# Two-pass scores on the full array, values of a token tile in one row, compression in one row with its weights in the stream's buffers

## The chip, the cores and the metric

One core of a Trainium2 chip runs the whole kernel in one launch. The metric is the device time in microseconds (us): the median of several executions, smaller is better. The engines named here are TensorE (PE, with its weight loads as PEld), VectorE (DVE), ScalarE (ACT) and SyncE (SP), which issues the DMAs of the weights.

## What is computed

Two layers of a decoder trunk on 256 tokens of width 1024, in float32. Each layer projects the normalized tokens with one wide matrix `w_in`, lets two attention mixers (NSA and DSA) work on the result, adds their output to the residual, and ends with a SwiGLU block. Cut to what the change touches:

```python
def layer(x):                                   # SEQ 256, D 1024, twice
    proj = rmsnorm(x) @ w_in                    # nsa_q, k/v for cmp/slc/win, dsa q/k/v, index q/k, gates
    # NSA: 8 heads of 64 in 2 groups; rope on q and keys
    kc = gelu(blocks(k_cmp) @ cmpk_w1 + b1) @ cmpk_w2 + b2   # 15 blocks of 32 tokens, w1: 2048 x 128
    vc = gelu(blocks(v_cmp) @ cmpv_w1 + b1) @ cmpv_w2 + b2
    o_c, o_s, o_w = softmax(q @ kc.T) @ vc, softmax(q @ k_slc.T) @ v_slc, softmax(q @ k_win.T) @ v_win
    # DSA: index scores pick 64 keys for each token, then 8 heads of 64
    sel = topk(sum(relu(iq @ ik.T) * iw), 64)
    o_d = softmax(dsa_q @ dsa_k[sel].T) @ dsa_v[sel]
    x = x + (gate_n * (o_nsa @ w_branch_nsa) + gate_d * (o_d @ w_branch_dsa)) @ w_out
    h = rmsnorm(x)
    return x + (silu(h @ w_ffn_gate) * (h @ w_ffn_up)) @ w_ffn_down
```

## The kernel before

**Weight stream.** All large matrices pass through `weights()` (L158 to L168). SP loads a piece of 128x1024 floats (512 KB) into `raw`, a pool of five buffers; ACT rounds it into `hi` (L164), DVE subtracts it from the piece into `lo` (L165), both in pools of four. `mul3` (L173 to L175) then multiplies each half of the split weights in three passes (hi by hi, hi by lo, lo by hi): twelve matmuls of 512 columns for a piece, L173, L174 and L175 in turn. A `raw` buffer comes free when its `lo` has been made. SP issues in one queue, in the order of the program, so an issue that waits holds back all behind it.

**Order.** A scheduler lays the matmuls of the attention between those of the stream. In each layer the order of the stream around the change is: index queries and keys, keys and values of NSA, queries of NSA (`nq`, column 0 of `w_in`), then the DSA queries (dq, four pieces of `w_in`), the DSA keys (dk, four), the DSA values (dv, four), then the gates.

**Scores.** `split` writes the hi part of queries and keys into plane 0 and the lo part into plane 1 of `qs` and `ks` (L315 to L318). `pair` (L320 to L325) computes two heads at a time, one on rows 0 to 63 of the array and one on rows 64 to 127: three passes each, so six matmuls that contract over 64 rows, of 256 columns (index scores, DSA, the first token tile of NSA) or 512 (second tile of NSA).

**Values.** `values` in `nsa` (L595) and in `dsa` (L636) multiplies the transposed weights `pt` with the values, 64 columns of the array for each of two heads. With `LAG = 1` the values of one group of heads are issued after the softmax of the next one.

**Compression.** The hidden layer of both compressions (L505) goes through four strips of 32 columns of the array (keys and values, first and second half of the contraction). Eight loads of 256 KB `w1` (L503) have a pool of their own of three buffers; after each come four matmuls on one strip. `blk`, the gathered blocks, comes from the NSA projections.

Of the kernel before, what the change touches and what calls it, by code (L numbers as in the profile page):

```python
# [9 lines left out]
F32 = mybir.dt.float32  # L10
# [19 lines left out]
WARM = 11  # L30
LAG = 1
HALF = (slice(0, 64), slice(64, 128))
PTB = 5

# [45 lines left out]
def hybrid_trunk(ctx: ExitStack, tc: tile.TileContext, a: dict, out: bass.AP):  # L80
# [233 lines left out]

    def split(dst, src):  # L315

        nc.scalar.activation(dst[0], src, AF.Copy)
        nc.vector.tensor_sub(dst[1], src, dst[0].bitcast(F32))  # L318

    def pair(outs, q, k):  # L320


        for n, (a, b) in enumerate(((0, 0), (0, 1), (1, 0))):
            for e in range(2):
                nc.tensor.matmul(outs[e], q[a][HALF[e]], k[b][HALF[e]], start=n == 0, stop=n == 2)  # L325

# [16 lines left out]
    for l in range(DEPTH):  # L343
# [16 lines left out]

        ks = one.tile([P, 2, NT, 2 * P], F32R, tag="ks", name="ks")
        qs = one.tile([P, 2, 4, SEQ], F32R, tag="qs", name="qs")
# [26 lines left out]
        iqs = one.tile([P, 2, 4, SEQ], F32R, tag="qs", name="iqs")[:, :, :, 0:P]  # L389
        iks = one.tile([P, 2, NT, 2 * P], F32R, tag="ks", name="iks").rearrange("p a b t -> p a (b t)")[:, :, 0:SEQ]  # L390
        for i in range(NT):
            nc.vector.tensor_scalar_mul(iw[:, i], pji[:, i, 576:584], 512 ** -0.5)
            rope(pji[:, i, 0:576].rearrange("p (h d) -> p h d", d=64), i, (9,))
            nc.vector.tensor_copy(pji[:, i, 576:640], pji[:, i, 512:576])
            tok = slice(i * P, (i + 1) * P)
            qp = tr_bank()
            for k in range(4):
                nc.tensor.transpose(qp[:, k * P:(k + 1) * P], pji[:, i, k * P:(k + 1) * P], ident)
            q3 = qp.rearrange("p (k t) -> p k t", t=P)
            if i == 0:  # L400
                iqT = work.tile([P, 4, P], F32, tag="pr", name="iqT", bufs=8)
                nc.scalar.activation(iqT, q3, AF.Copy)
            else:
                split([iqs[:, a] for a in range(2)], q3)
            kp = tr_bank()[:, 0:P]
            nc.tensor.transpose(kp, pji[:, i, 512:640], ident)
            nc.scalar.activation(iks[:, 0, tok], kp, AF.Copy)
            if i == 0:
                nc.scalar.activation(ikT, kp, AF.Copy)
            nc.vector.tensor_sub(iks[:, 1, tok], kp, iks[:, 0, tok].bitcast(F32))  # L410
        for i in range(NT):
# [4 lines left out]
            for p0 in range(0, 4, per):  # L416
                sbs = [sc_bank() for _ in range(2)]
                for p in range(p0, p0 + per):
                    outs = [sb[:, (p - p0) * nk:(p - p0 + 1) * nk] for sb in sbs]
                    if i == 0:  # L420
                        for e in range(2):
                            nc.tensor.matmul(outs[e], iqT[HALF[e], p], ikT[HALF[e]], start=True, stop=True)
                    else:
                        pair(outs, [iqs[:, z, p] for z in range(2)], [iks[:, z] for z in range(2)])
                for e in range(2):
                    rl = work.tile([P, 512], F32, tag="k2", name="rl", bufs=3)
                    nc.scalar.activation(rl, sbs[e], AF.Relu)
                    for p in range(p0, p0 + per):
                        h = 2 * p + e
                        nc.vector.scalar_tensor_tensor(acc, rl[:, (p - p0) * nk:(p - p0 + 1) * nk],  # L430
                                                       iw[:, i, h:h + 1], prev, ALU.mult, ALU.add)
                        prev = acc
# [13 lines left out]
        for c0, n in ((512, 512), (1024, 280), (0, 512)):  # L446
            d = project(act, w_in, c0, n)
            for i in range(NT):
                if c0 == 0:
                    nq[i] = work.tile([P, 512], F32, tag="q2", name="nq", bufs=4)  # L450
                    evac(nq[i].rearrange("p (r g d) -> p r g d", r=4, g=2),
# [5 lines left out]
        for i in range(NT):  # L457
# [13 lines left out]
            for k, c in enumerate((C_KSLC, C_KWIN)):  # L471
                nc.tensor.transpose(kp[:, k * P:(k + 1) * P], pj[:, i, c - C0:c - C0 + P], ident)
            split([ks[:, z, i] for z in range(2)], kp[:, 0:2 * P])
            tok = slice(i * P, (i + 1) * P)
# [4 lines left out]
            nc.scalar.activation(qT[:, :, tok], q3, AF.Copy)  # L479
            split([qs[:, z, :, tok] for z in range(2)], q3)  # L480
            nc.scalar.activation(eg[:, i], pj[:, i, C_NG - C0:C_NG - C0 + 24], AF.Exp, scale=-1.0)
            nc.vector.tensor_scalar(eg[:, i], eg[:, i], 1.0, None, ALU.add)


        hp = sc_bank()
        for kind, nm in ((0, "cmpk"), (1, "cmpv")):
            blk = work.tile([P, 16, 32], F32, tag="pr", name="blk", bufs=8)
# [3 lines left out]
            for half in range(2):  # L491
                src = kvP[:, kind].rearrange("p g (c m) -> p m g c", m=8)[:, :, :, half:half + 15]
                po = cols[:, pos + half * 8:pos + half * 8 + 8].unsqueeze(2).broadcast_to((P, 8, 15))
                for g in range(2):
                    nc.vector.tensor_add(blk4[:, half * 8:(half + 1) * 8, g, 0:15], src[:, :, g], po)
            for half in range(2):
                q = 32 * (2 * half + kind)
                for mq in range(2):
                    r0 = half * 1024 + mq * 512
                    w1 = work.tile([P, 4, P], F32, tag="w1", name="w1", bufs=3)  # L500
                    if l == 0 and kind == 0 and half + mq < 2:
                        after(w1[:, 0, 0:1], pji[:, 0, 0:1])
                    nc.sync.dma_start(w1, a[nm + "_w1"][l, r0:r0 + 512].rearrange("(m p) h -> p m h", p=P))  # L503
                    for m in range(4):
                        nc.tensor.matmul(hp[q:q + 32, 0:P], blk[:, half * 8 + mq * 4 + m], w1[:, m],  # L505
                                         start=mq == 0 and m == 0, stop=mq == 1 and m == 3, tile_position=(0, q))
        hs = work.tile([P, P], F32, tag="hs", name="hs", bufs=1)
# [31 lines left out]
        for c0, dst in ((C_DQ, dqT), (C_DK, dkT), (C_DV, None)):  # L539
            d = project(act, w_in, c0, 512)  # L540
            for i in range(NT):
                if dst is None:
                    evac(dv[:, i], d[i], rstd[i])
                    continue
                q = work.tile([P, 512], F32, tag="q2", name="dq", bufs=4)
                evac(q, d[i], rstd[i])
# [11 lines left out]
        def nsa(i):  # L558
# [30 lines left out]

            def values(r0, pts):  # L590
                for r in range(r0, r0 + per):
                    for kind, vcol in ((0, C_VSLC - C0), (1, C_VWIN - C0)):
                        for b in range(i + 1):
                            for g in range(2):
                                nc.tensor.matmul(yn[g * 64:(g + 1) * 64, r * P:(r + 1) * P],  # L595
                                                 pj[:, b, vcol + g * 64:vcol + g * 64 + 64],
                                                 pts[g][:, ((r - r0) * 2 + kind) * (i + 1) + b],
                                                 start=r == 0 and kind == 0 and b == 0, stop=False)

            done = []  # L600
            for r0 in range(0, 4, per):
# [3 lines left out]
                for r in range(r0, r0 + per):  # L605
                    pair([o[r - r0] for o in outs], [qs[:, z, r, tok] for z in range(2)],
                         [ks[:, z, 0:i + 1].rearrange("p b t -> p (b t)") for z in range(2)])
                for g in range(2):
# [6 lines left out]
                done.append((r0, pts))  # L615
                if len(done) > LAG:
                    values(*done.pop(0))
            for d in done:
                values(*d)
            for r in range(4):  # L620
# [4 lines left out]
        def dsa(i):  # L625
# [4 lines left out]

            def values(p0, pts):
                for p in range(p0, p0 + per):
                    for b in range(i + 1):
                        for e in range(2):
                            v0 = (2 * p + e) * 64
                            nc.tensor.matmul(yd[e * 64:(e + 1) * 64, p * P:(p + 1) * P], dv[:, b, v0:v0 + 64],  # L636
                                             pts[e][:, (p - p0) * (i + 1) + b], start=p == 0 and b == 0,
                                             stop=p == 3 and b == i)

            done = []  # L640
            for p0 in range(0, 4, per):
                pts = []
                sbs = [sc_bank() for _ in range(2)]
                for p in range(p0, p0 + per):
# [4 lines left out]
                    else:  # L649
                        pair(outs, [dqs[:, z, p] for z in range(2)], [dks[:, z, p] for z in range(2)])  # L650
                for sb in sbs:
                    segs = sb.rearrange("p (h b t) -> p h b t", h=per, t=P)
                    pts.append(softmax([segs[:, h] for h in range(per)], dbias[i], None))
                done.append((p0, pts))
                if len(done) > LAG:
                    values(*done.pop(0))
            for d in done:
                values(*d)
            y_out(yd, 4, tok)
# [4 lines left out]
        dks = one.tile([P, 2, 4, SEQ], F32R, tag="qs", name="dks")  # L664
        dqs = one.tile([P, 2, NT, 2 * P], F32R, tag="ks", name="dqs").rearrange("p z b (c t) -> p z (b c) t", t=P)
        split([dks[:, z] for z in range(2)], dkT)
        split([dqs[:, z] for z in range(2)], dqT[:, :, P:])
        dsa(0)
# [190 lines left out]
```

## Time and profile before

| | |
|---|---|
| median of 3 runs | 834.9 us (834.82 to 835.3) |
| profiled execution | 835.01 us, span of its trace 833.0 us |
| mean granted TensorE clock | 0.999 |
| PE busy | 824.6 us, 99% of the span |
| DVE busy | 534.0 us, 64% |
| ACT busy | 452.4 us, 54% |
| PE's share of the chain that ended last | 98% |

The span is what the trace covers; 2.0 us of the profiled execution lie outside it. Busy shares are averages over the span; a row of the timeline is one instruction, or several alike in a row, with its start and its length. Ends of matmuls are modelled, so lengths of neighbours overlap, and what an instruction costs PE is read from start to start.

### The profile page before, as it was taken

Reading aid. Unit: us, or ns where it says so; the run is one execution under the profiler, and the core shown is the slowest. Engines: PE = TensorE matmul, PEld = TensorE weight load, DVE = VectorE, ACT = ScalarE, POOL = GpSimd, SP = SyncE. Lnnn points to the kernel's source line nnn. Section 1 sums busy time; section 2 is a strip of 40 time slices with the busy share of each in tenths; the row PEclk is TensorE's granted clock in tenths of the full one; section 3 lists DMA queues with packets and bytes.
Section 4 is the critical chain, followed back from the end, with each engine's and each line's share of the span. In section 5 each row is a group of like instructions: output and inputs, shape, how many; then the busy total and the mean of one; then the engine's idle time right before and its main releaser. Section 6 shows DMA issues by size and latency. Waiting matters only on the chain.

```text
span 833.0 us, 12280 instructions
## 1 busy us (share of the span) xinstructions
PE 824.6 (99%) x4501; PEld 680.1 (82%) x4501; DVE 534.0 (64%) x1163; ACT 452.4 (54%) x777; POOL 8.4 (1%) x18
## 2 busy tenths in 40 slices
PE   8999999999999999999999999999999999999997
PEld 7878887778888888988898888777788888889886
DVE  6699478868665556554668956767577555556445
ACT  6754467854565444533567545667546554544433
POOL 0100000000000000000000000000000000000000
PEclk9999999999999999999999999999999999999999
DMA  8955653225475664576376565332254755546651
GB/s 275 335 166 183 190 176 102 89 70 180 143 226 164 192 189 140 185 237 188 87 233 189 166 190 176 117 88 78 86 183 153 215 185 182 181 126 224 210 177 51
DMA packets 76331, 140.08 MB, mean 168 GB/s; under 512 B 5056, under 2 KB 24512, under 8 KB 76272
## 3 DMA queue, kind: packets, MB, share of 16 engines
q1 hardware_dynamic: 76032, 138.59, 53.5%
q0 software_dynamic: 240, 0.72, 0.4%
q8 instruction: 35, 0.57, 0.3%
q14 instruction: 24, 0.20, 0.1%
HBM read 138.24 MB, written 1.05 MB: 167 GB/s over the span
## 4 chain that ended last, share of the span: by engine, by line
PE 98%; DMA 1%; SPq 0%; ACT 0%; DVE 0%; issue 0%; POOLq 0%; ACTq 0%
PE mm L174 26%; PE mm L173 26%; PE mm L175 26%; PE sc L325 3%; PE tr L280 3%; PE yv L595 2%; PE sc L505 2%; PE yv L175 1%; PE yv L174 1%; PE yv L173 1%; PE tr L784 1%; PE yv L636 1%; DMA raw<-w_in 1%; PE tr L234 1%; PE yv L621 1%; PE sc L174 0%
## 5 line engine op out<-in xcount | busy, mean ns | idle before, releaser
L165 DVE TENSOR_TENSOR lo<-raw,hi 128x1024 fp32r<-128x1024 f32 (+3 forms) x264 | 302.2, 1149 | 174.6 <-ACT hi L164 170.4
L164 ACT ACTIVATE hi<-raw 128x1024 fp32r<-128x1024 f32 (+3 forms) x264 | 261.9, 999 | 209.4 <-PE mm L175 142.3
L174 PE MATMUL mm<-lo,ah 128*128 128x512 f32 (+3 forms) x850 | 319.9, 377 | 0.0
L173 PE MATMUL mm<-hi,ah 128*128 128x512 f32 (+3 forms) x850 | 318.7, 380 | 0.0
L175 PE MATMUL mm<-hi,al 128*128 128x512 f32 (+3 forms) x850 | 318.0, 376 | 0.0
L174 PEld LDWEIGHTS mm<-lo,ah 128*128 128x128 f32 x850 | 160.0, 188 | 29.4 <-issue 2.8
L175 PEld LDWEIGHTS mm<-hi,al 128*128 128x128 f32 x850 | 159.6, 188 | 28.7 <-issue 1.2
L173 PEld LDWEIGHTS mm<-hi,ah 128*128 128x128 f32 x850 | 159.7, 188 | 28.2 <-issue 0.7
L174 PE MATMUL mm<-lo,hh 128*128 128x512 f32 x126 | 49.3, 391 | 0.0
L175 PE MATMUL mm<-hi,hl 128*128 128x512 f32 x126 | 49.1, 390 | 0.0
L173 PE MATMUL mm<-hi,hh 128*128 128x512 f32 x126 | 48.7, 395 | 0.0
L300 ACT ACTIVATE pr<-pr,mx 128x128 f32<-128x128 f32 (+1 forms) x96 | 42.5, 445 | 10.4 <-DVE mx L297 10.3
L789 DVE TENSOR_TENSOR hl<-tr,hh 128x512 fp32r<-128x512 f32 (+1 forms) x24 | 15.5, 647 | 36.0 <-ACT hh L788 36.0
L788 ACT ACTIVATE hh<-tr 128x512 fp32r<-128x512 f32 (+1 forms) x24 | 13.5, 562 | 44.6 <-PE tr L784 44.6
L175 PEld LDWEIGHTS mm<-hi,hl 128*128 128x128 f32 x126 | 23.7, 188 | 4.9
L174 PEld LDWEIGHTS mm<-lo,hh 128*128 128x128 f32 x126 | 23.7, 188 | 4.1
L173 PEld LDWEIGHTS mm<-hi,hh 128*128 128x128 f32 x126 | 23.7, 188 | 4.1
L309 DVE TENSOR_SCALAR pr<-pr,c 128x128 f32<-128x128 f32 (+1 forms) x96 | 25.3, 316 | 1.0
L281 ACT COPY pt<-tr 128x512 f32<-128x512 f32 x36 | 20.4, 583 | 9.7 <-PE tr L280 9.6
L297 DVE CUSTOM_DVE_ANT_0 pr<-sc,cst 128x128 f32<-128x128 f32 (+1 forms) x64 | 19.1, 354 | 6.8 <-PE sc L325 6.8
L280 PE MATMUL tr<-cst,pr 128*128 128x128 f32 x144 | 22.3, 278 | 0.0
L775 ACT ACTIVATE sg<-mm,rstd 128x512 f32<-128x512 f32 (+1 forms) x24 | 15.7, 654 | 8.8 <-PE mm L175 8.6
(242 smaller groups left out, 777.2 us busy)
## 6 DMA issues: line engine op xcount, KB each, us to landing
raw<-w_in SPq DMA_DIRECT2D x72, 512.0 KB, 3.5
raw<-w_ffn_down SPq DMA_DIRECT2D x44, 512.0 KB, 4.4
raw<-w_ffn_gate SPq DMA_DIRECT2D x40, 512.0 KB, 4.2
raw<-w_ffn_up SPq DMA_DIRECT2D x40, 512.0 KB, 4.3
raw<-w_out SPq DMA_DIRECT2D x16, 512.0 KB, 3.5
raw<-w_in SPq DMA_DIRECT2D x16, 292.0 KB, 3.5
raw<-w_branch_nsa SPq DMA_DIRECT2D x16, 256.0 KB, 4.0
raw<-w_branch_dsa SPq DMA_DIRECT2D x8, 512.0 KB, 3.5
```

The costliest lines, as they stand in the source:

```text
L164: nc.scalar.activation(hi[:, 0:kt * n], raw[:, 0:kt * n], AF.Copy)
L165: nc.vector.tensor_sub(lo[:, 0:kt * n], raw[:, 0:kt * n], hi[:, 0:kt * n].bitcast(F32))
L173: nc.tensor.matmul(dst, xh, wh, start=first, stop=False)
L174: nc.tensor.matmul(dst, xh, wl, start=False, stop=False)
L175: nc.tensor.matmul(dst, xl, wh, start=False, stop=last)
L280: nc.tensor.transpose(tp[:, k * P:(k + 1) * P], piece, ident)
L281: nc.any.tensor_copy(dst, tp[:, 0:len(parts) * P].rearrange("p (k t) -> p k t", t=P))
L297: nc.vector.tensor_tensor_reduce(pr[:, h].rearrange("p (b t) -> p b t", t=P), v, b3, -0.125, 3.4e38, ALU.add, ALU.min, accum_out=mx[:, h:h ...
L300: nc.scalar.activation(pr[:, h], pr[:, h], AF.Exp, bias=mx[:, h:h + 1], scale=-1.0, accum_out=sm[:, h:h + 1])
L309: nc.vector.tensor_scalar_mul(pr[:, h], pr[:, h], c[:, h:h + 1])
L325: nc.tensor.matmul(outs[e], q[a][HALF[e]], k[b][HALF[e]], start=n == 0, stop=n == 2)
L505: nc.tensor.matmul(hp[q:q + 32, 0:P], blk[:, half * 8 + mq * 4 + m], w1[:, m], start=mq == 0 and m == 0, stop=mq == 1 and m == 3, tile_pos ...
```

## The change

- **Scores.** `pair` and `split` go. `stack` lays hi of one head into its 64 rows and lo of the same head into the other 64; `twice` lays hi of a head into both halves of one plane and lo into both halves of another. `score` then contracts over all 128 rows in two passes: (hi+lo) by hi, and (hi+lo) by lo. In NSA the queries are stacked and the keys doubled (`ks` grows from two planes to four), in DSA the keys are stacked and the queries doubled. The index scores stack the queries; their keys stood in both halves already.
- **Values.** `LAG` and both `values` functions go. After all softmaxes of a token tile, all its value products stand in one hand-ordered row (`manual_schedule`), the last heads first. Five buffers of `pt` become eight.
- **Compression.** Four loads of 512 KB instead of eight of 256 KB, into `raw` buffers; the pool `w1` goes. All 32 matmuls stand in one hand-ordered row after them, the four strips in turn. The buffers of `q2` go from four to three.

```diff
-LAG = 1
-PTB = 5
+PTB = 8
...
-    def pair(outs, q, k):
-        for n, (a, b) in enumerate(((0, 0), (0, 1), (1, 0))):
-            for e in range(2):
-                nc.tensor.matmul(outs[e], q[a][HALF[e]], k[b][HALF[e]], start=n == 0, stop=n == 2)
+    def stack(dst, src):
+        for e in range(2):
+            nc.scalar.activation(dst[e][HALF[e]], src[HALF[e]], AF.Copy)
+        for e in range(2):
+            nc.vector.tensor_sub(dst[e][HALF[1 - e]], src[HALF[e]], dst[e][HALF[e]].bitcast(F32))
+    def twice(dh, dl, src):
+        for e in range(2):
+            nc.scalar.activation(dh[e][HALF[e]], src[HALF[e]], AF.Copy)
+            nc.any.tensor_copy(dh[e][HALF[1 - e]], src[HALF[e]])
+        for e in range(2):
+            for h in (e, 1 - e):
+                nc.vector.tensor_sub(dl[e][HALF[h]], src[HALF[e]], dh[e][HALF[e]].bitcast(F32))
+    def score(o, q, k):
+        pairs = [(q, t) for t in k] if isinstance(k, (list, tuple)) else [(t, k) for t in q]
+        for n, (u, v) in enumerate(pairs):
+            nc.tensor.matmul(o, u, v, start=n == 0, stop=n == 1)
...
-                    w1 = work.tile([P, 4, P], F32, tag="w1", name="w1", bufs=3)
-                    nc.sync.dma_start(w1, a[nm + "_w1"][l, r0:r0 + 512].rearrange("(m p) h -> p m h", p=P))
-                    for m in range(4):
-                        nc.tensor.matmul(hp[q:q + 32, 0:P], blk[:, half * 8 + mq * 4 + m], w1[:, m],
-                                         start=mq == 0 and m == 0, stop=mq == 1 and m == 3, tile_position=(0, q))
+        strips = [(half, kind) for half in range(2) for kind in range(2)]
+        for half, kind in strips:
+            w1 = wraw.tile([P, 1024], F32, tag="raw", name="w1").rearrange("p (m h) -> p m h", h=P)
+            src = a[("cmpk_w1", "cmpv_w1")[kind]][l, half * 1024:(half + 1) * 1024]
+            nc.sync.dma_start(w1, src.rearrange("(m p) h -> p m h", p=P))
+            w1s.append(w1)
+        with tc.manual_schedule(engines={nc.tensor.engine}):
+            for m in range(8):
+                for (half, kind), w1 in zip(strips, w1s):
+                    q = 32 * (2 * half + kind)
+                    nc.tensor.matmul(hp[q:q + 32, 0:P], blks[kind][:, half * 8 + m], w1[:, m],
+                                     start=m == 0, stop=m == 7, tile_position=(0, q))
...
-                if len(done) > LAG:
-                    values(*done.pop(0))
-            for d in done:
-                values(*d)
+            with tc.manual_schedule(engines={nc.tensor.engine}):
+                for n, (r, kind, b, g) in enumerate((r, kind, b, g) for r in range(3, -1, -1) for kind in range(2)
+                                                    for b in range(i + 1) for g in (1, 0)):
+                    r0, pts = done[r // per]
+                    vcol = (C_VSLC, C_VWIN)[kind] - C0 + g * 64
+                    nc.tensor.matmul(yn[g * 64:(g + 1) * 64, r * P:(r + 1) * P], pj[:, b, vcol:vcol + 64],
+                                     pts[g][:, ((r - r0) * 2 + kind) * (i + 1) + b], start=n < 2, stop=False)
```

The same lines of code sit up to 12 lines lower in the changed kernel (the load of a piece is its L161, the compression L522, the values L630 and L665, the scores L334).

SP's queue in layer 0, from the last piece of `nq` on. Before, the loads of `w1` stand between the pieces; in `raw_877` to `raw_931` are dq's four, in `raw_979` dk's first. DVE in brackets is the wait for the `lo` that frees a buffer.

```order
L162 DMA raw_688<-w_in 128x2x512 [waits DMAHW6_49,DVE_49]
L162 DMA raw_877<-w_in 128x2x512 [waits DMAHW7_49,DVE_49]
L162 DMA raw_895<-w_in 128x2x512 [waits DMAHW0_49,DVE_49]
L162 DMA raw_913<-w_in 128x2x512 [waits DMAHW1_49,DVE_49]
L162 DMA raw_931<-w_in 128x2x512 [waits DMAHW3_49,DMAHW2_49,DVE_49]
L162 DMA raw_979<-w_in 128x2x512 [waits DMAHW6_49,DVE_49]
```

Now, from the last piece of `nq` (`raw_682`) to dk's fourth (`raw_1035`); PE in brackets is the wait for matmuls.

```order
L161 DMA raw_682<-w_in 128x2x512 [waits DMAHW6_49,DMAHW3_49,DVE_49]
L516 DMA w1_809<-cmpk_w1 128x8x128 [waits DMAHW7_49,DVE_49]
L516 DMA w1_811<-cmpv_w1 128x8x128 [waits DMAHW0_49,DVE_49]
L516 DMA w1_813<-cmpk_w1 128x8x128 [waits DMAHW1_49,DVE_49]
L516 DMA w1_815<-cmpv_w1 128x8x128 [waits DMAHW2_49,DVE_49]
L161 DMA raw_879<-w_in 128x2x512 [waits DMAHW3_49,DVE_49]
L161 DMA raw_897<-w_in 128x2x512 [waits DMAHW0_49,DVE_49]
L161 DMA raw_915<-w_in 128x2x512 [waits DMAHW1_49,DVE_49]
L161 DMA raw_933<-w_in 128x2x512 [waits DMAHW2_49,DVE_49]
L161 DMA raw_981<-w_in 128x2x512 [waits DMAHW4_49,DMAHW3_49,DVE_49]
L161 DMA raw_999<-w_in 128x2x512 [waits DMAHW5_49,PE_49]
L161 DMA raw_1017<-w_in 128x2x512 [waits DMAHW6_49,PE_49]
L161 DMA raw_1035<-w_in 128x2x512 [waits DMAHW7_49,PE_49]
```

The four `w1` loads take four of the five buffers ahead of dq. The five pieces `raw_879` to `raw_981` (dq's four and dk's first) have all been given the one buffer that is left, as the addresses of the built program show, and each waits for the `lo` of the one ahead of it. The next three wait for the compression's matmuls. Layer 1 has the same order.

PE's queue at the values of the first token tile of NSA in layer 0, before: the row from one burst of values to the next, with scores and transposes around them.

```order
L280 MATMUL tr<-cst,pr 128x128 x4
L595 MATMUL yv<-pt,ga 64x128 x8
L280 MATMUL tr<-cst,pc 128x128
L325 MATMUL sc<-ks,qs 128x512 x6
L175 MATMUL mm<-hi,al 128x512
...
L595 MATMUL yv<-pt,ga 64x128 x7
L621 MATMUL yv<-pct,gb 128x128 x4
L280 MATMUL tr<-cst,pr 128x128 x8
L325 MATMUL sc<-ks,qs 128x512 x6
```

The same place now:

```order
L174 MATMUL mm<-hi,al 128x512
L630 MATMUL yv<-pt,ga 64x128 x16
L633 MATMUL yv<-pct,gb 128x128 x4
L279 MATMUL tr<-cst,pr 128x128 x8
L334 MATMUL sc<-ks,qs 128x512 x4
L172 MATMUL mm<-hi,ah 128x512
```

The sixteen products of the tile, three bursts before (one, eight and seven), are one, and six matmuls of a score burst are four.

## Rows read from the trace of the kernel before

**Rows 1.** Page: span, busy time of the engines, clock in 40 slices.
```profile
span 833.0 us, 12280 instructions
...
PE 824.6 (99%) x4501; PEld 680.1 (82%) x4501; DVE 534.0 (64%) x1163; ACT 452.4 (54%) x777; POOL 8.4 (1%) x18
...
PEclk9999999999999999999999999999999999999999
```

**Rows 2.** The chain that ended last, shares of the span, by engine and line.
```profile
PE 98%; DMA 1%; SPq 0%; ACT 0%; DVE 0%; issue 0%; POOLq 0%; ACTq 0%
by line: PE mm L174 25.8%; PE mm L173 25.7%; PE mm L175 25.7%; PE sc L325 2.9%; PE tr L280 2.7%; PE yv L595 1.9%; PE sc L505 1.6%; PE yv L175 1.5%; PE yv L174 1.5%; PE yv L173 1.5%; PE tr L784 1.2%; PE yv L636 0.9%; DMA raw<-w_in 0.7%; PE t
```

**Rows 3.** Timeline of PE: score bursts and their neighbours; start, length, engine, line.
```profile
119.62 0.39 PE L175 MATMUL mm<-hi,al 128*128 128x512 f32 x1
119.93 1.32 PE L325 MATMUL sc<-ks,qs 64*128 64x256 f32 x12
121.19 0.50 PE L173 MATMUL mm<-hi,ah 128*128 128x512 f32 x1
121.52 0.40 PE L174 MATMUL mm<-lo,ah 128*128 128x512 f32 x1
```

**Rows 4.** Timeline of PE: stream matmuls of 512 and 256 columns (one of 512 left out).
```profile
340.12 0.39 PE L174 MATMUL mm<-lo,ah 128*128 128x512 f32 x1
...
340.57 0.28 PE L173 MATMUL mm<-hi,ah 128*128 128x256 f32 x1
340.69 0.28 PE L174 MATMUL mm<-lo,ah 128*128 128x256 f32 x1
```

**Rows 5.** Timeline of PE: bursts of values, and the score burst behind one.
```profile
134.60 0.43 PE L595 MATMUL yv<-pt,ga 128*64 128x128 f32 x2
134.96 0.98 PE L325 MATMUL sc<-ks,qs 64*128 64x512 f32 x6
135.87 0.50 PE L174 MATMUL mm<-lo,ah 128*128 128x512 f32 x1
...
139.50 1.09 PE L595 MATMUL yv<-pt,ga 128*64 128x128 f32 x16
140.52 0.33 PE L280 MATMUL tr<-cst,pc 128*128 128x128 f32 x1
```

**Rows 6.** Timeline of PE: a burst of the compression; an fp32 matmul has two records.
```profile
73.86 2.40 PE L505 MATMUL sc<-w,blk 128*32 128x128 f32 x24
76.19 0.66 PE L280 MATMUL tr<-cst,dq 128*128 128x128 f32 x4
```

**Rows 7.** Groups by form, 28 to 112 us: busy, mean ns, idle before.
```profile
L165 DVE TENSOR_TENSOR lo<-raw,hi 128x1024 fp32r<-128x1024 f32 x23 | 28.1, 1224 | 11.2 <-ACT hi L164 10.7
L164 ACT ACTIVATE hi<-raw 128x1024 fp32r<-128x1024 f32 x23 | 24.2, 1058 | 19.6 <-PE mm L175 16.5 <-issue 2.6 <-ACT kcbd L528 0.4
```

**Rows 8.** Loads of the stream, 40 to 80 us, from issue to landing.
```profile
DMA to landing us min/median/max: 3.3/3.4/6.0
```

**Rows 9.** Busy time by window: length, then PE, PEld, DVE, ACT, POOL, clock, DMA.
```profile
55.00:80.00 25.00, 25.00 (x151) 20.49 (x146) 24.82 (x85) 12.47 (x18) 0.00 (x0) 1.00 0.55 170
80.00:112.00 32.00, 32.00 (x169) 25.62 (x168) 15.33 (x28) 14.86 (x21) 0.00 (x0) 1.00 0.64 195
```

**Rows 10.** Timeline of DVE: lo of nq's last piece in each layer.
```profile
42.53 1.21 DVE L165 TENSOR_TENSOR lo<-raw,hi 128x1024 fp32r<-128x1024 f32 x1
...
451.26 1.22 DVE L165 TENSOR_TENSOR lo<-raw,hi 128x1024 fp32r<-128x1024 f32 x1
```

**Rows 11.** Timeline of PE: first matmul of dq in each layer.
```profile
55.32 0.48 PE L173 MATMUL mm<-hi,ah 128*128 128x512 f32 x1
...
462.00 0.48 PE L173 MATMUL mm<-hi,ah 128*128 128x512 f32 x1
```

**Rows 12.** Timeline of PE: the kernel's first matmuls.
```profile
1.19 4.50 PE L112 MATMUL tr<-zeros 128*128 128x512 bf16 x11 [1.19 <-DVE warm L118]
```

## What the change does to the time, foretold

> **What bounds the kernel now.** I read the page first. PE is busy 824.6 of 833.0 us, its granted clock stands at full in all forty slices, and no other engine is above 64% [rows 1]. The chain that ended last says the same in another way: 98% of it is PE, and behind the stream's three lines come the ones that the change touches, the scores (L325, 2.9% of 833.0, so 24.2 us), the values (L595 and L636, 1.9% and 0.9%, 23.3 us) and the compression (L505, 1.6%, 13.3 us) [rows 2]. So PE work that goes is time won, unless PE then waits for weights. Then I read PE's timeline for what each burst costs from start to start, the stream's rows for what one piece costs on its way to PE, and the windows for how busy DVE is there.
>
> **Scores.** Two stream matmuls of 512 columns take 0.45 us from start to start (340.12 to 340.57), 0.225 each, and those of 256 columns start 0.12 apart [rows 4]. Six half-row matmuls of 512 columns take 0.91 us (134.96 to 135.87), 0.15 each, where half of 0.225 would be 0.11 [rows 5]. Going into a burst from the stream costs some 0.08 more (119.62 to 119.93 is 0.31), and the first stream matmul behind it takes 0.33, 0.10 more [rows 3]. There are 29 bursts, 20 of them followed by the stream, so L325 with its changes of shape costs 24.2 + 29x0.08 + 20x0.10 = 28.5 us. After, 128 full-row matmuls do it, 96 of 256 and 32 of 512 columns: 96x0.12 + 32x0.225 = 18.7, with no change of the array's shape; 0.3 for odd starts. **Saved: 9.5 us.** Bounds: 4.3, if the full-row bursts pay the same 0.18, and 10.5, if bursts before cost 0.03 more than these rows show.
>
> Here a rule speaks against the change. The Trainium skill, "TensorEngine Tiling (Array Packing)", section Performance Considerations, recommends two-fold row tiling for a contraction of 64 or less, and its Overview gives up to 2x. By it the 192 half-row passes would be 96 full slots of work, fewer than the 128 that replace them; the page prices neither the entry nor the exit of a burst but says under Key Properties that a change of tiling mode drains the engine. By 2x without that drain the old scores would cost 72x0.12 + 24x0.225 = 14.0 us and the change would lose 4.7. The rows contradict the 2x (0.15, not 0.11) and show the drain (0.18 a burst), so the sum goes by them.
>
> **Values.** The products stay the same, 144 slots of two column halves. A burst of 16 records (8 slots) takes 1.02 us, one of 2 (1 slot) 0.36 [rows 5]: (1.02 - 0.36)/7 = 0.094 a slot and 0.27 a burst, and going in costs 0.08 as above. With 33 bursts that gives 144x0.094 + 33x0.27 = 22.4, near the 23.3 of the chain. After there are 8 bursts (order of PE: 16, 32, 8 and 16 matmuls in each layer), 25 fewer: **saved 25x0.35 = 8.8 us.** Bounds: 6, if a long row still pays for its inner changes of bank, and 9.5. The hand-ordered row stands some 20 stream matmuls behind the last scores, as the last burst did before, so I cost its wait at nothing; without that cover it would be the softmax, a few us once or twice.
>
> **Compression.** One burst of 24 records takes 2.33 us (73.86 to 76.19), 0.097 a record, one strip at a time [rows 6]. After, 64 records a layer go through four strips in turn. Not overlapped they take 6.2 us a layer; two in a slot, as the column halves of the values do, 64/2x0.094 = 3.0; four in a slot 1.5. No row shows four; I take 2.3 between the last two, plus 0.2 for the change of shape: 5.0 in both layers. Before, 13.3 + 8 bursts x 0.18 = 14.7. **Saved: 9.7 us**, bounds 1.9 and 11.3.
>
> PE work saved: 9.5 + 8.8 + 9.7 = 28.0 us.
>
> **The stream's buffers.** This is where it is given back. Before, five `raw` buffers run ahead and PE never waits: 25.00 of 25 us busy from 55 on [rows 9]. Now the four `w1` hold four of them until the compression, which PE reaches behind dq's four pieces, and SP gives dq's four pieces and dk's first the fifth, one after the other; all later issues stand behind them in SP's queue. A cycle of that one buffer is the landing 3.4 [rows 8] + hi 1.06 + lo 1.22 [rows 7] + 0.1 = 5.8 us, while PE needs 12x0.225 = 2.7 for a piece. The first issue comes with the end of the `lo` of `nq`'s last piece: 42.53 + 1.21 = 43.7 and 451.26 + 1.22 = 452.5 [rows 10]. So dk's first piece is ready at 43.7 + 5c and 452.5 + 5c, where c is the mean cycle. Without waits PE would be there at 55.3 [rows 11] - 0.9 (gained by then on index scores, an estimate) + 4x2.7 + 3x0.64 (transposes, as 76.19 [rows 6]) + 2.5 (compression) = 69.6, and at 462.0 - 0.9 + 15.2 = 476.3. PE's waits are the difference: (43.7 + 452.5 + 10c) - (69.6 + 476.3) = 10c - 49.7.
>
> With c = 5.8, the floor: 8.3 us. But hi and lo stand in line: DVE is busy 24.82 of 25 us in this stretch [rows 9], with rows that belong to the NSA projections and `blk`, and `stack` and `twice` add to it. By columns and the 1.22 us for 1024 [rows 7] their further subtracts are 1536 (`ks`) + 1024 (`qs`) + 512 (index) + 1024 + 1536 (DSA) = 5632 columns a layer, 6.7 us if 64 partitions take as long as 128, the first 3000 of them here. Five `lo` instead of nine in the stretch give some of it back. I take c = 6.5, a `lo` held up by one DVE row of the common size; upper end 3.4 replaced by the slowest landing 6.0: c = 8.4, or 34.3 us of waits. **Given back: 10x6.5 - 49.7 = 15.3 us.** The three pieces after dk's first come into buffers that the compression frees, all three at once, and cover each other; from 80 on DVE has 15.33 of 32 us of work [rows 9], which hides the rest of the added subtracts, at nothing. If that cover were gone, 3.7 us a layer would come.
>
> The eight 256 KB loads become four of 512 KB, the same bytes. `q2` with three buffers instead of four: dq's tiles wait for transposes that PE has done by then; nothing, or one transpose burst (0.64) in each layer.
>
> **Sum.** Against the profiled execution: span 833.0 - 28.0 + 15.3 = 820.3, and 2.0 outside it: 822. The median, 834.9, is 0.1 under the profiled 835.01, so it needs no correction.
>
> **Rivals.**
> A. The waits are smaller: the buffer turns at its floor or better, since DVE's rows can stand behind the `lo`. For: ACT is half idle there (12.47 of 25 busy [rows 9]) and five `lo` replace nine. Against: DVE is full. 833.0 - 28.0 + 8.3 + 2.0 = 815, 807 with no wait at all. 0.13.
> B, the other side: the one buffer turns so slowly that it eats the saving. Place: dq to dk's first; it decides at 10c - 49.7 = 28.0, c = 7.8, two us above the floor. For: landings up to 6.0 occur, DVE full, one `lo` may sit behind two subtracts of 1.2 us. With c = 8.2 the waits are 32 and the time 839. 0.10.
> C. The clock falls in PE's gaps. The kernel's first eleven matmuls of 512 columns, behind an idle start, take 4.50 us, 0.41 each, which is the 1.2 GHz level, against 0.225 at 2.4 GHz [rows 4, 12]: 2.2 us more for a piece. Within the stretch the waits would swallow that (12x0.41 = 4.9 is under c); two pieces a layer behind it would not: +8.8, 831. Against: the page shows full clock throughout, but also no gap. 0.06. The Trainium skill, "TensorE: Matmul & The Clock Gate", Part 1, describes such a gate: idleness throttles, activity releases it. No row before shows gaps between pieces.
> D. The compression doesn't do what it says: four strips run one after the other, 6.4 us a layer. It saves 1.9, the sum is 830. Against: column halves of the values do overlap. 0.05.
> E. Half-row pairs were the better form, by the page's 2x: 4.7 lost instead of 9.5 saved, 836. Against it stand the rows. 0.02.
>
> **How the numbers follow.** The forecast has 0.64, its own range 817 to 827 (c from 6.0 to 7.0, savings by 2 us either way). A measurement here tells about 0.2%, 1.7 us, from no change. Faster: forecast, A, C and D, less 0.03 for sums that land at the old time: 0.85; same 0.03; slower B and E, 0.12. The range of 8 in 10 goes from 811, inside A, to 833, short of B: 811 to 833.
>
> **What would show it.** PE rows of scores 0.12 and 0.225 apart with no 0.18 around them; eight bursts of values; a compression burst near 2.3 us a layer; PE idle for some 15 us in all, in two stretches (about 55 to 75, and 455 to 482), ended by hi or lo with the DMA of `w_in` behind it; full PE elsewhere. Idle PE at the value rows, or a lower granted clock behind the gaps, would make it wrong, and so would a cycle of the single buffer outside 6 to 7 us.

## The result, and the profile after

The changed kernel takes 823.7 us (median of 4 runs, 822.47 to 826.47) against 834.9 before: a ratio of 0.987, 95% interval 0.984 to 0.989, so 11.2 us faster. The prediction was 822, range 811 to 833. The profiled execution is the slowest of the four (826.47 us, span 824.7), so its sums lie 2.8 us above the median.

Page of the changed kernel, the lines that answer to [rows 1], and the chain by engine, which answers to [rows 2]:

```profile
span 824.7 us, 12192 instructions
...
PE 803.2 (97%) x4437; PEld 674.5 (82%) x4437; DVE 548.4 (66%) x1191; ACT 462.9 (56%) x798; POOL 8.4 (1%) x18
...
PEclk9998999999999999999999979999999999999999
...
PE 88%; DVE 7%; DMA 3%; issue 1%; ACT 1%; SPq 0%; POOLq 0%; ACTq 0%
```

PE is busy for 21.4 us less, the span is only 8.3 shorter, and two slices of the clock are no longer 9. The chain has gone from 98% PE to 88%: DVE and the DMA of the stream are on it now. Where, the windows tell (length; PE, PEld, DVE, ACT, POOL; clock, DMA share, GB/s), as in [rows 9]:

```profile
55.00:80.00 25.00, 17.91 (x143) 13.04 (x142) 24.39 (x80) 13.65 (x23) 0.00 (x0) 0.93 0.41 131
80.00:112.00 32.00, 32.00 (x157) 26.44 (x156) 23.82 (x65) 17.81 (x31) 0.00 (x0) 0.94 0.69 210
455.00:490.00 35.00, 29.22 (x190) 21.80 (x189) 31.38 (x99) 17.91 (x27) 0.00 (x0) 0.85 0.45 148
```

PE is idle for 7.1 us in the first and 5.8 in the third, 12.9 in all, and for nothing anywhere else between 40 and 780 us; before, it was idle for nothing there. These are the dq and dk stretches of the two layers. What it waits for most, from the view of waits (in total, times, longest):

```profile
PE mm L173 <- DVE lo L164: 7.3, 4, 4.1
PE mm L172 <- ACT hi L163: 4.1, 4, 1.4
```

The DMA view of 43 to 84 us shows the one buffer at work, in 40 slices of about 1 us: a piece lands in about three slices, then nothing moves for three, four times over, until the compression frees the other four buffers at 74 us.

```profile
GB/s 149 327 186 294 46 0 0 0 82 344 86 0 0 0 190 312 10 0 0 0 148 330 50 0 0 0 74 352 94 0 0 164 358 368 338 378 408 404 244 316
```

The new bursts on PE's timeline: eight index scores, the compression's row (64 records), the values of one token tile, and what follows each. A bracket at the end of a row is the time that PE stood idle before it, with what ended the wait.

```profile
48.85 1.11 PE L334 MATMUL sc<-iks,iqs 128*128 128x256 f32 x8
49.80 0.40 PE L173 MATMUL mm<-lo,ah 128*128 128x512 f32 x1
...
71.71 2.43 PE L522 MATMUL sc<-w,blk 128*32 128x128 f32 x64
74.07 0.73 PE L172 MATMUL mm<-hi,ah 128*128 128x512 f32 x2
78.86 0.79 PE L173 MATMUL mm<-lo,ah 128*128 128x512 f32 x1 [4.06 <-DVE lo L164]
79.45 0.63 PE L174 MATMUL mm<-hi,al 128*128 128x512 f32 x1
79.88 0.63 PE L172 MATMUL mm<-hi,ah 128*128 128x512 f32 x1
...
134.06 1.97 PE L630 MATMUL yv<-pt,ga 128*64 128x128 f32 x32
135.96 0.60 PE L633 MATMUL yv<-pct,gb 128*128 128x128 f32 x3
```

Scores: 0.95 us for eight, 0.12 each, and the next stream matmul comes without a longer step [rows 4]. Compression: 2.36 us for 64 records, where 24 took 2.33 [rows 6]. Values: 1.90 for 16 slots. Behind the compression PE does two passes with `hi` and then waits 4.06 us for a `lo`; the stream matmuls after that wait start 0.43 us apart (79.45 to 79.88), the lower clock. DVE has the reason for that `lo`:

```profile
72.63 1.39 DVE L319 TENSOR_TENSOR qs<-tr,qs 64x512 fp32r<-64x512 f32 x2
...
75.17 1.73 DVE L328 TENSOR_TENSOR ks<-tr,ks 64x256 fp32r<-64x256 f32 x4
...
77.58 1.22 DVE L164 TENSOR_TENSOR lo<-raw,hi 128x1024 fp32r<-128x1024 f32 x1
```

Its `hi` had been ready at 73.78. From then to 77.58 DVE did the end of a `stack`, the four subtracts of a `twice` (1.73 us) and rows of the rope and the selection, which the change doesn't touch. Dk's first piece is ready at 78.80 in layer 0 and 484.57 in layer 1; the one buffer was first filled from 43.86 and 450.87 on. That is a cycle of 7.0 and 6.7 us.

My theory at this point: the work saved is about what was predicted, and the one buffer gives back 12.9 us as idle time and some 5 more as slow matmuls behind it. The rival: VectorE's added subtracts hold up the stream, whatever the buffers.

### The profile page after: what moved, and what is told of

It reads as the page before. It is cut to its first block, busy times and chain, and to the rows that moved or that the text cites. A ratio compares the mean times of both kernels' runs of the same rounds, so it can differ in the third digit from the quotient of the medians.

```text
span 824.7 us, 12192 instructions
## 1 busy us (share of the span) xinstructions
PE 803.2 (97%) x4437; PEld 674.5 (82%) x4437; DVE 548.4 (66%) x1191; ACT 462.9 (56%) x798; POOL 8.4 (1%) x18
## 4 chain that ended last, share of the span: by engine, by line
PE 88%; DVE 7%; DMA 3%; issue 1%; ACT 1%; SPq 0%; POOLq 0%; ACTq 0%
PE mm L173 24%; PE mm L172 24%; PE mm L174 24%; DMA raw<-w_in 3%; PE tr L279 2%; PE sc L334 2%; DVE lo L164 2%; PE yv L173 1%; PE yv L172 1%; PE yv L174 1%; PE yv L630 1%; PE tr L793 1%; DVE ga L449 1%; ACT hi L163 1%; PE yv L665 1%
## 5 line engine op out<-in xcount | busy, mean ns | idle before, releaser
L172 PE MATMUL mm<-hi,hh 128*128 128x512 f32 x126 | 48.7, 395 | 0.0
L279 PE MATMUL tr<-cst,pr 128*128 128x128 f32 x144 | 20.1, 273 | 0.0
```

The source lines that it names most:

```text
L172: nc.tensor.matmul(dst, xh, wh, start=first, stop=False)
L279: nc.tensor.transpose(tp[:, k * P:(k + 1) * P], piece, ident)
```

## The experiments

Each was timed in four or more runs beside the kernel before on the same chip (834.7 to 834.9 us). The name in brackets is that of the kernel in the tables and in the text behind.

**One part at a time.** The first three put one part of the change into the kernel before; their edits are the three bullets of the change, each with its piece of the diff. Where room was short, `q2` has three buffers and, with the value rows, `w1` two.

> The two-pass scores alone, put into the kernel before, with three buffers of q2 to make room. Theory: the 9.5 us of the prediction's first term come out whole, because the stream keeps five buffers and hides the added subtracts of VectorE: 825 to 827 us, no idle TensorE between 55 and 90. Rival: the added work of stack and twice is what holds the pieces up, whatever the buffers: 830 or more, with TensorE waiting for lo.

Measured (scores_only): **821.0 us** (0.983, 0.982 to 0.985), 13.9 faster. No idle PE: 25.00 of 25 us in 55 to 80, with DVE busy 24.61. So the stream with five buffers carries the added subtracts, and the rival falls. The gain is 4.4 above the term, so the theory's range is missed; why is taken up below.

> The value rows alone, in the kernel before (three buffers of q2, two of w1 to make room). Theory: 25 fewer bursts at 0.35 us, 8.8 us, so 825 to 827. Rival: a hand-ordered row has to wait for its last softmax and gives back most of it: 831 to 836, with idle TensorE just ahead of L595's and L636's rows.

Measured (values_only): **831.3 us** (0.996, 0.994 to 0.997), 3.6 faster: the theory's range is missed, and the time is in the rival's. But PE is not idle ahead of any value row, so the rival's reason is not it.

> The compression alone, in the kernel before: row of 32, weights in the stream's buffers, no stack or twice on VectorE. Theory: the work falls by 10 us, but dq's pieces and dk's first still pass through one buffer (cycle about 6.3 us, a little less than with the scores' subtracts), so some 8 us of idle TensorE and some 4 us at the lower clock come back: 834 to 838, no gain, perhaps a loss. Rival: the subtracts of the scores are the cause and the one buffer would do without them: 825 to 828.

Measured (compress_only): **835.2 us** (1.000, 0.999 to 1.001; ten runs), no change, as the theory had it. PE is idle for 6.9 us in the same two stretches, and the clock is 0.93 in 55 to 80 (seven matmuls 0.43 us apart, so some 1.4 us, not the 4 expected). Two more waits, of 0.76 us each at 207.84 and 616.71, are for `ah`, the hi part of the activations, and stand in the kernel with the late compression too. The compression as it was changed is worth nothing by itself.

**The same work, with the buffers held for a short time.** The loads, the row and what hangs on it move behind dk, where the gathered blocks have long been ready; the changed kernel otherwise.

```diff
+        def compression():
+            strips = [(half, kind) for half in range(2) for kind in range(2)]
...
         for c0, dst in ((C_DQ, dqT), (C_DK, dkT), (C_DV, None)):
+            if dst is None:
+                compression()
             d = project(act, w_in, c0, 512)
```

> The changed kernel, with the four w1 loads, the row of 32 and what hangs on it moved behind dk, so that dq and dk pass through all five buffers and the gathered blocks are ready before the weights of the compression land. Same work on all engines. Theory: the idle TensorE (12.9 us more than before) and the stretches at a lower clock (6 to 7 us) both vanish: 805 to 809 us, granted clock 0.99 or more in every stretch from 55 to 112. Rival: VectorE's added work is the cause: 816 to 822, with waits for lo at the same places.

Measured (late_dv, called the late kernel from here on): **806.6 us** (0.966, 0.965 to 0.968), inside the theory's range and faster than both kernels. Its windows:

```profile
55.00:80.00 25.00, 25.00 (x141) 19.82 (x139) 24.69 (x76) 14.09 (x23) 0.00 (x0) 1.00 0.41 122
80.00:112.00 32.00, 32.00 (x204) 26.70 (x203) 26.10 (x86) 21.26 (x47) 0.00 (x0) 1.00 0.79 247
455.00:490.00 35.00, 35.00 (x231) 27.80 (x230) 30.95 (x85) 21.31 (x32) 0.00 (x0) 1.00 0.61 193
```

No idle time, full clock, VectorE as full as in the changed kernel. So 823.7 - 806.6 = 17.1 us were given back by the place of the loads and of the row that they feed, and 834.9 - 806.6 = 28.4 are what the three parts are worth.

The same move with the compression alone:

> The compression alone, as one row over four strips, in the kernel before, but with its loads and its row behind dk as in the late kernel. The prediction's term is 9.7 us: 825.1. If the three parts add up to the late kernel's gain of 28.4 (13.9 for the scores alone, 3.6 for the values alone), 10.9 are left for it: 823.9. Rival: it brings 12 or more, because two-pass scores and value rows take some of its gain away: 822 or less; or under 8, 827 or more, because they add to it.

Measured (late_compress_only): **824.95 us** (0.989, 0.987 to 0.990), 9.7 faster: the term, to the tenth (how much of that is luck is said below). With compress_only it says that the place of the loads costs some 10 us there, without any work on VectorE from the scores.

**How much is held, and how long.** Two versions between those ends: `w1` in two pairs, and all four ahead of dk instead of dq (the second diff is against the late kernel; `hidden` holds what hangs on the row).

```diff
+        def strip_rows(half):
+            w1s = []
+            for kind in range(2):
...
+        strip_rows(0)
...
         for c0, dst in ((C_DQ, dqT), (C_DK, dkT), (C_DV, None)):
+            if dst is dkT:
+                strip_rows(1)
+                hidden()
```

```diff
-            if dst is None:
+            if dst is dkT:
                 compression()
```

> The changed kernel with w1 in two pairs: the loads of the first half ahead of dq, those of the second behind dq's pieces. So dq has three buffers and only dk's first three pieces turn in one. Theory, the loss grows with the pieces that turn in one buffer: no idle TensorE in dq, some in dk: 808 to 816. Rival, any w1 in the stream's buffers costs the same: 821 to 825.

> The changed kernel with all four w1 loads behind dq's pieces and ahead of dk's. Four buffers are held, but only from when dq's pieces have left them to the row, some 10 us instead of 25, and three pieces turn in the fifth. Theory: idle TensorE of a few us only, 807 to 814. Rival, four buffers held cost what they cost in the changed kernel, wherever they stand: 821 to 825.

Measured (two_and_two and late_dk): **813.4** (0.974, 0.972 to 0.975) and **811.4 us** (0.971, 0.970 to 0.972), both as their theory had it. PE is idle for 2.8 and 4.4 us. So it is pieces turning in one buffer, five, three or none of them in a layer, and not `w1` in the stream's buffers as such. Two_and_two has 1.6 us less idle time and is still 2.0 slower than late_dk. Its two rows alternate two strips, 6.76 us of compression against 4.56, which takes more than the 1.6 back; the rest of the difference I didn't separate.

**The clock.** 18 matmuls that nobody reads, behind the row in layer 0:

```diff
+            if l == 0:
+                idle = sc_bank()
+                for m in range(18):
+                    nc.tensor.matmul(idle, act[0][:, 0, 0:P], act[0][:, 0:2].rearrange("p k t -> p (k t)"),
+                                     start=True, stop=True)
```

> The changed kernel with 18 matmuls of 512 columns on data that nobody reads, behind the compression's row of layer 0 alone. They fill the wait of 4.06 us ahead of the lo of dk's first piece. Theory, the clock follows idleness: the ten matmuls behind the wait, 0.43 us apart in the changed kernel, come at 0.23, so some 2 us are gained although work is added: 820.5 to 823, with layer 1 unchanged. Rival, the slow matmuls come from the four loads that land at the same time (335 GB/s between 75 and 80 us): they stay slow and the time is that of the changed kernel, 823 to 826, or more.

Measured (after_fill): **822.4 us** (0.985, 0.983 to 0.987). The timeline of this kernel at the place shown above:

```profile
73.07 4.38 PE L527 MATMUL sc<-ah 128*128 128x512 f32 x18
77.28 0.61 PE L172 MATMUL mm<-hi,ah 128*128 128x512 f32 x2
77.86 0.50 PE L173 MATMUL mm<-lo,ah 128*128 128x512 f32 x1
78.19 0.39 PE L174 MATMUL mm<-hi,al 128*128 128x512 f32 x1
78.42 0.40 PE L172 MATMUL mm<-hi,ah 128*128 128x512 f32 x1
```

The matmuls behind the filled wait start 0.23 us apart instead of 0.43 (78.19 to 78.42), with the same four loads landing. The windows say the same: the first line is the changed kernel, the second this one, with more bytes moving and the full clock.

```profile
75.00:80.00 5.00, 1.14 (x3) 0.96 (x4) 4.88 (x17) 1.93 (x2) 0.00 (x0) 0.67 1.00 335
75.00:80.00 5.00, 5.00 (x22) 3.86 (x21) 4.93 (x16) 1.73 (x2) 0.00 (x0) 1.00 1.03 385
```

From 80 to 85 the clock is 0.65 and 1.00. So it follows the idle engine and not the loads. The time is 1.3 us lower, which the intervals don't separate. Layer 1, left as it was, has six matmuls at 0.43 in this profile and 14 in that of the changed kernel, so the slow stretches differ from run to run, and only layer 0 speaks for the filling.

**VectorE's part in the cycle.**

```diff
-            for h in (e, 1 - e):
-                nc.vector.tensor_sub(dl[e][HALF[h]], src[HALF[e]], dh[e][HALF[e]].bitcast(F32))
+            nc.vector.tensor_sub(dl[e][HALF[e]], src[HALF[e]], dh[e][HALF[e]].bitcast(F32))
+        for e in range(2):
+            nc.scalar.activation(dl[e][HALF[1 - e]], dl[e][HALF[e]].bitcast(F32), AF.Copy)
```

> The changed kernel with two of the four subtracts of twice replaced by copies on ScalarE, so that VectorE has about 0.9 us less for each token tile ahead of a lo. Theory, VectorE's rows ahead of lo are what lifts the cycle of the one buffer from its floor of 5.8 us to 6.9: mean cycle down by 0.3 to 0.4, the idle time of TensorE from 12.9 to 9 to 11 us, 819 to 822. Rival, the landings set the cycle: 823 to 825.

Measured (after_light): **823.1 us** (0.986, 0.984 to 0.987), no difference that can be told from 823.7, and in the rival's range. The idle time falls from 12.9 to 10.8 us, but the cycle doesn't. In layer 0 five cycles run from 44.84 to 79.13, 6.9 us each. In layer 1 only four pieces turn in the one buffer, from 450.42 to 478.38, 7.0 each; the fifth is issued as the compression's row ends, ahead of the fourth one's `lo`, so it goes into another buffer:

```profile
475.50 0.37 SPq L161 DMA_DIRECT2D raw<-w_in  x1
477.17 1.21 DVE L164 TENSOR_TENSOR lo<-raw,hi 128x1024 fp32r<-128x1024 f32 x1
480.14 1.22 DVE L164 TENSOR_TENSOR lo<-raw,hi 128x1024 fp32r<-128x1024 f32 x1
```

So this edit leaves the theory unproven. What VectorE does to the cycle is seen from each piece's landing, `hi` and `lo`. Over the ten pieces (dq's four and dk's first in both layers) `lo` stands 7.3 us behind other rows of VectorE once its `hi` is ready in the changed kernel, 7.8 here, and 2.2 in compress_only, which has no rows of `stack` and `twice`. Landings take 3.7 to 3.9 us on average in all three. The cycle of compress_only is 6.5 us (43.62 to 76.06 for five, 457.01 to 482.82 for four), so the scores' rows add some 0.4 to it, by one profile of each kernel.

**What the strips and the order are worth**, each in the late kernel: the strips one after the other, the values as before, the scores as before (these two by taking back their piece of the diff).

```diff
-                for m in range(8):
-                    for (half, kind), w1 in zip(strips, w1s):
+                for (half, kind), w1 in zip(strips, w1s):
+                    for m in range(8):
```

> The kernel with the late compression, its 32 matmuls ordered strip by strip instead of the four strips in turn. Theory, the strips work at the same time only where they follow each other: 64 records at 0.1 us in a layer instead of 2.5 us, 4 us more in each, 813 to 816. Rival, the gain comes from the row and the missing changes of shape alone: 806 to 808.

Measured (late_strips): **813.7 us** (0.974, 0.973 to 0.976), 7.2 slower than the late kernel, in the theory's range. One strip after the other, 30 records take 2.58 us (first line to the second); in turn, 50 take 1.65 (third to the fourth, of the late kernel):

```profile
81.98 2.65 PE L523 MATMUL sc<-w,blk 128*32 128x128 f32 x30
84.56 0.66 PE L279 MATMUL tr<-cst,dq 128*128 128x128 f32 x4
```
```profile
80.20 1.72 PE L523 MATMUL sc<-w,blk 128*32 128x128 f32 x50
81.85 0.50 PE L172 MATMUL mm<-hi,ah 128*128 128x512 f32 x1
```

So 0.086 us a record and 0.033: the four strips work at the same time.

> The kernel with the late compression, but the values in the old order (LAG 1, five buffers of pt). Beside two-pass scores the rows are worth what the bursts of the kernel with the scores alone cost more, 20.3 less 16.9 us, plus some of the changes of shape: 810 to 812. Rival, the prediction's 8.8 us hold once the scores don't change the shape: 815. Second rival, the 3.6 us of the value rows alone: 810.

> The kernel with the late compression, but the half-row scores of before. If the prediction's 9.5 us are what two passes are worth by themselves, 815 to 817. Rival: they are worth the 13.9 us that they brought alone, 819 to 822; then the order of the program has no part in it.

Measured (late_novalues and late_noscores): **813.3** (0.974, 0.973 to 0.975) and **818.9 us** (0.980, 0.979 to 0.982). The first lies between the theory's 810 to 812 and the rival's 815, the second just below its rival's 819 to 822, so neither theory held. Beside the two other parts the value rows are worth 6.7 us and the two-pass scores 12.3. Neither is the prediction's term, and for the values neither is the number that they brought alone.

## Why the prediction held, point by point

**The sum of the saved work** was right: 28.0 foretold, 28.4 measured. Its parts were not: alone they brought 13.9, 3.6 and 9.7 us where 9.5, 8.8 and 9.7 were foretold, so that the sum met is luck in part. Time on PE from each instruction's start to the next one's, waits included, summed by kind from the traces (us); a change of shape is one between neighbours on PE that use different parts of the array (128*128, 64*128, 128*64 or 128*32 in a row):

| | before | scores_only | values_only | late_compress_only | late_dv |
|---|---|---|---|---|---|
| scores | 24.5 | 20.2 | 25.8 | 24.8 | 19.7 |
| values | 23.2 | 20.3 | 16.9 | 21.0 | 16.9 |
| compression | 13.7 | 14.3 | 14.9 | 5.1 | 5.1 |
| transposes | 48.7 | 46.5 | 48.7 | 50.7 | 46.1 |
| stream | 702.1 | 697.4 | 701.7 | 700.4 | 695.5 |
| bursts of scores / of values | 29 / 33 | 31 / 22 | 34 / 8 | 29 / 24 | 32 / 8 |
| changes of the tile's shape | 153 | 84 | 118 | 132 | 54 |

*Scores*, 9.5 foretold, 13.9 alone, 12.3 beside the others. The bursts themselves gave 4.4 and the stream around them 4.7, together 9.1, near the term (in the trace of before 24 of the 29 bursts are followed by the stream, not 20, a matter of 0.4 us). What the term lacked is in other kinds: values 2.9 and transposes 2.3. It took the rest of the program as fixed, but the order of PE now has 22 bursts of values instead of 33. Why the scheduler laid them so isn't shown: with the scores of before, late_compress_only has 24.

*Values*, 8.8 foretold, 3.6 alone, 6.7 beside the others. The bursts gave 6.2 of the 6.8 (25 x 0.27) that the in-burst part of the term had. The 0.08 for going in, 25 times, was not there: the stream gave back 0.4 only, perhaps because most bursts stood beside transposes and scores, which kept their own changes (18 of the 33 were entered from these, 24 left to something other than the stream). And scores and compression grew by 2.5, with 34 score bursts for 29 (the compression perhaps by its two buffers of `w1`, which I didn't separate). Rows and counts alone can't tell who pays for a change of shape between two neighbours; I had charged it to both.

*Compression*, 9.7 foretold, 9.7 measured in late_compress_only. The value between two and four strips in a slot (5.0 us in all) stands against 5.1 in the late kernel and 4.4 in the changed one. The compression's own time fell by 8.6 us and the stream around it by 1.7, near the two parts of the term. That the whole is 9.7 is luck: values gave another 2.2, in 24 bursts, and transposes took 2.0, of which 1.5 are the two waits for `ah`.

**What is given back**, 15.3 foretold, 17.1 measured between the medians of the changed and the late kernel. The mechanism was right in each place: one buffer, SP's queue behind it, two stretches, ended by hi or lo, nothing elsewhere. That the sizes met is luck, for three errors offset each other.

- The cycle was 6.9 us, not 6.5, by which 10c - 49.7 gives 19.
- The idle time was 12.9 all the same. In layer 1 the buffer was first filled 1.6 us earlier than the sum had it (450.87, not 452.5). And PE, its idle time taken out, came to the `lo` of dk's first piece at 71.8 and 478.9, together 4.8 us later than the sum's 69.6 and 476.3. Some 0.9 of these are passes with `hi` that PE does ahead, which the formula left out; in layer 1 the low clock has a part; the rest I can't split.
- Some 4.8 us came as rival C: 24 stream matmuls of the profiled execution start 0.41 to 0.43 us apart, 0.2 more than at full clock. The sum had this term at nothing. I had put it behind the stretch and given it a chance of 0.06 as a case by itself; it is part of the likeliest one. The prediction named a lower granted clock behind the gaps among the signs that would make it wrong, and that sign came.

The idle 12.9 and the 4.8 are of the profiled execution. Its span exceeds that of the late kernel by 20.6 us, so 2.9 of it are in neither.

The Trainium skill, "TensorE: Matmul & The Clock Gate", Part 1, has idleness throttle the engine, and the rows agree: behind waits of 1.90 and 4.06 us the spacing goes to 0.43, and filled with work it stays 0.23. Not every wait did it: behind 0.90 us up to 62.82 and 1.44 up to 67.93 it stays 0.23.

**The tiling rule.** By the 2x of "TensorEngine Tiling (Array Packing)" in the Trainium skill the scores would have lost 4.7 us (rival E). Scores_only shows 13.9 gained. The rows have two reasons. The half-row bursts of before take 24.5 us where the 2x would give 14.0: twelve matmuls of 256 columns take 1.26 us, 0.105 each, where a full-row one takes 0.12 [rows 3, 4]. And with 69 changes of shape fewer the stream gives back 4.7 us. The same page of the Trainium skill, Key Properties, names a drain on a change of mode, and the 4.7 agree with it; how much of them is the drain no run separates. Its Overview gives up to 4x for 32 columns: the rows show 0.086 / 0.033 = 2.6 for four strips.

Rivals A and D are out by these runs (12.9 us idle; strips at 0.033 us a record). B needed a cycle of 7.8; the formula behind that point is too strict, as shown. What stays open in part is the spread of the changed kernel, 822.5 to 826.5 us in four runs where before spread over 0.5 beside it. The mean granted clock of these runs, from the fastest to the slowest, is 0.997, 0.993, 0.993 and 0.987, so the time at the lower clock goes with it. It is not all: the four runs of after_light spread over 3.0 us at 0.991 to 0.992, and those of the late kernel over 1.5 at 0.998 to 0.999.

## What to carry to other kernels

Buffers borrowed from a stream cost by the pieces that must turn in what is left: here 17.1 us for five pieces a layer, 4.8 for three in late_dk, nothing that shows for none. So put the borrower's loads where its other operand is ready, so that they leave as soon as they land. When PE is the bound, count the changes of tile shape over the whole program after scheduling, with the order built, rather than a price for each burst; a change in one part moves its neighbours as well. A stall of PE can cost more than its idle time, since the matmuls behind it may run at half the clock for a while (some 4.8 us here beside 12.9 idle).

## What the runs showed of the hardware that was not expected

Four column strips fed in turn take 0.033 us a record, fed one by one 0.086 (late_dv and late_strips).

The clock also fell behind short waits. In layer 1 of the changed kernel PE waits 0.89 us up to 468.52 and 1.90 us up to 471.38; the timeline of PE from there:

```profile
471.38 0.50 PE L173 MATMUL mm<-lo,ah 128*128 128x512 f32 x1 [1.90 <-DVE lo L164]
...
472.43 0.44 PE L174 MATMUL mm<-hi,al 128*128 128x512 f32 x1
472.67 0.63 PE L173 MATMUL mm<-lo,ah 128*128 128x512 f32 x1
473.09 0.63 PE L174 MATMUL mm<-hi,al 128*128 128x512 f32 x1
...
478.12 0.39 PE L173 MATMUL mm<-lo,ah 128*128 128x512 f32 x1
478.35 0.40 PE L174 MATMUL mm<-hi,al 128*128 128x512 f32 x1
```

The first matmuls behind the wait still start 0.24 us apart (472.43 to 472.67), the next ones 0.42 (472.67 to 473.09); at 478 they are back at 0.23, with PE busy in between. The granted clock is 1.00 from 466 to 472.6 and 0.50, the 1.2 GHz level, from 472.7 to 476. So what these waits cost in clock comes after them, on work that waits for nothing.
